# Strassen's weight sums: made once in the mix phase and kept in memory, instead of three times in the up-projection

## The chip, the cores and the metric

The kernel runs on one core of a Trainium2 chip. The time is the device time of one launch in microseconds, taken as the median of a few runs. The profile comes from one further execution that was recorded by the hardware profiler.

## The reference

One decoder layer runs on 2048 prompt positions and 64 sample positions (8 sequences of 8), D_MODEL 1024. The input is normalised and projected; three branches (windowed attention, a spatial-gating MLP, cross-attention into a memory) are each mapped back to 1024 channels, gated and summed; then a ConvFFN follows: an up-projection to 2 x 2816 channels, a causal convolution of width 3 over the positions, a gated GELU, and a down-projection.

```python
gate_logits = ...                                   # 3 x 1024 of the input projection
proj = einsum('blnc,ncd->blnd', branches, w_o)
x = x + rms_norm(sum(sigmoid(gate_logits) * proj, axis=2), post_mix_g)
h = rms_norm(x, pre_ffn_g)
up = einsum('bld,df->blf', h, w_up)                 # 1024 -> 5632
ext = concatenate([conv_past, up], axis=1)
c = conv_b + sum(ext[:, j:j+L] * conv_w[j] for j in range(3))
gate, val = split(c, 2)
f = einsum('blf,fd->bld', gelu(gate) * val, w_down)
x = x + rms_norm(f, post_ffn_g)
```

All of it is in float32. For a product to be as exact as that, each operand is split into a high and a low part, and three matmuls (high x high, high x low, low x high) stand for one.

## The kernel before

The program has four stages, one after the other: stage 1 (branches), the mix phase (gates, branch outputs and their sum), the up phase and the down phase. The 2112 positions are handled in three token groups g of T2 = 704, and 704 is two halves of CW = 352. `split` (L69 to L72) makes the two parts of an operand: ACT casts the source to the high part (L71), and VectorE subtracts that from the source to get the low part (L72).

**Mix phase** (`mix_phase`). For each token group, `proj0` projects branch 0 with four weights; then `branches` goes over n = 0, 1, 2 and op = 0 to 3: two gate weights, and for n > 0 one projection weight, are loaded by `load_w` (512 KB each, DMA issued on the queue of SyncE, SP; split on ACT and VectorE; four weight buffers, three buffers for what is loaded). A gate gemm is 48 matmuls for each half of an `op`, a projection gemm 24, so an `op` has 96 matmuls of 128x352 for n = 0 and 144 for n > 0. `load_br` loads and splits the four tiles of a branch (`bx`), and `post_mix` normalises the sum, adds it to x and stores it.

**Up phase** (`up_phase`). One step of Strassen's algorithm (Winograd's form) halves the rows of the weight, the columns of the weight and the positions, so 7 products do the work of 8. A `Quad` is one (g, f) of 3 token groups and 22 pairs of feature tiles: 66 quads, each of 7 products, each product of 12 matmuls 128x352. For each token group `build_ops` (L915 to L940) loads the activations, scales them on VectorE (L928), makes the four sums t1 to t4 on GpSimd (L936) for each of 4 j, and splits 7 operands for each j: 28 tiles, of 32 buffers. For each quad `build_w` (L942 to L959) loads the raw weight in one DMA of 1024 KB, GpSimd makes the four sums s1 to s4 (L954), and all seven are split: 7 casts on ACT, 7 subtractions on VectorE (tiles `wa` for the raw ones, `ws` for the sums). So each weight is read, summed and split three times, once for each token group.

The products gather in PSUM banks x and y (two buffers each) and w (one). ACT copies partial results out of them (L988 p1, p5, u2, u3; L1024 the last product), `plus` (L1013) adds them up into the tile e: u3 + p5 on GpSimd, the others on VectorE. `conv` (L1042, L1046) does the convolution of the gate half and the value half: one ACT operation and two of VectorE on 704 positions for each; then come Gelu on ACT (L1054), the product on VectorE (L1057) and the store to `act_d`. These run in `act`, called by `end`, and the loop calls `q.first()`, `prev.end()`, `q.middle()`, so that one quad's last product comes after the next one's first.

The order of the instructions on each engine is set by the tile framework's scheduler when the program is built, from the order of the code, the buffers and priorities.

## Time and profile before

| What | Value |
|---|---|
| median of 3 runs | 3266.31 us (3262.56 to 3273.02) |
| profiled execution | 3264.22 us, span of its instructions 3262.4 us |
| mean granted clock of TensorE | 0.965 |
| stages on the span | stage 1 to about 725 us, mix phase to 1680, up phase to 2706, down phase to 3262 |
| busy share | PE 93%, VectorE (DVE) 65%, ACT 43%, GpSimd (POOL) 36% |

A busy time is the sum of an engine's instructions; SP issues the DMAs. PEld is the load of weights into TensorE, which runs beside the matmuls. The granted clock is the share of full speed that the throttle let TensorE have in a stretch. "x" numbers are counts of instructions.

### The profile page before, as it was taken

The numbers are of one execution on the slowest core, as the hardware profiler recorded it, in microseconds if no ns is written. First come the engines' busy times: TensorE is split into PE (matmuls) and PEld (weight loads), VectorE is DVE, ScalarE is ACT, GpSimd is POOL, SyncE is SP. The second block draws the span as 40 slices with busy tenths as digits, with TensorE's granted clock in tenths as the row PEclk, the third lists the DMA queues.
The fourth block names the chain that finished last, engine by engine and source line by source line (L and its number), as shares of the span: only waits on it lengthen the run. The fifth ranks groups of instructions, "written<-read, shape, count | busy, mean of one in ns | idle before, by whom it ended". The sixth has DMA issues, their size and how long they took to land.

```text
span 3262.4 us, 50709 instructions
## 1 busy us (share of the span) xinstructions
PE 3031.9 (93%) x20060; PEld 2962.3 (91%) x20060; DVE 2114.6 (65%) x3013; ACT 1400.7 (43%) x2547; POOL 1185.4 (36%) x1062
## 2 busy tenths in 40 slices
PE   8999999989998999899939999899989997999997
PEld 8999999989998999899938998799979997999997
DVE  6666665544235423632289999999999995555553
ACT  5545564123223212322225555555555554444442
POOL 3221100000111111301167777777789981222221
PEclk9999999999999999899959999999999998999999
DMA  6222233224124212512142223322322226666662
GB/s 201 57 73 74 89 94 84 74 87 145 66 89 160 102 65 89 183 63 74 44 151 100 101 91 105 109 87 105 109 84 105 88 91 232 222 213 202 207 198 103
DMA packets 162894, 376.47 MB, mean 115 GB/s; under 512 B 21520, under 2 KB 94736, under 8 KB 154192
## 3 DMA queue, kind: packets, MB, share of 16 engines
q1 hardware_dynamic: 162656, 373.24, 34.5%
q8 instruction: 157, 2.57, 0.3%
q14 instruction: 81, 0.66, 0.1%
HBM read 315.17 MB, written 58.99 MB: 115 GB/s over the span
## 4 chain that ended last, share of the span: by engine, by line
PE 64%; DVE 21%; issue 8%; ACT 3%; DMA 2%; POOL 1%; SPq 0%; DVEq 0%; ACTq 0%; POOLq 0%
PE ps_g L740 16%; PE ps_d L1121 16%; DVE c L1046 7%; PE ps_p L740 6%; DVE ws L72 4%; PE ps_x L979 4%; PE ps_q L188 3%; PE ps_sv L188 3%; PE ps_up L202 2%; PE ps_mqp L202 2%; DVE wa L72 2%; PE ps_y L979 2%; PE ps_kv L188 1%; DVE m L868 1%; PE ps_w L979 1%
## 5 line engine op out<-in xcount | busy, mean ns | idle before, releaser
L740 PE MATMUL ps_g<-h,w_g 128*128 128x352 f32 x3456 | 570.9, 325 | 16.2 <-ACT m L833 16.2
L740 PEld LDWEIGHTS ps_g<-h,w_g 128*128 128x128 f32 x3456 | 563.0, 191 | 16.6 <-ACT m L833 16.6
L1121 PE MATMUL ps_d<-a,wd 128*128 128x352 f32 x3168 | 514.8, 324 | 16.9 <-ACT a L71 16.1
L1121 PEld LDWEIGHTS ps_d<-a,wd 128*128 128x128 f32 x3168 | 510.9, 190 | 18.2 <-ACT a L71 16.7
L1046 DVE SCALAR_TENSOR_TENSOR c<-e,k_conv_w,c 128x704 f32<-128x704 f32 (+1 forms) x264 | 347.3, 1317 | 10.4 <-ACT c L1042 9.1
L856 POOL TENSOR_TENSOR m<-m,sg 128x704 f32<-128x704 f32 x48 | 94.9, 1977 | 693.0 <-DVE sg L855 531.3
L72 DVE TENSOR_TENSOR ws<-s,ws 128x512 fp32r<-128x512 f32 x264 | 312.4, 1189 | 19.2 <-ACT ws L71 19.1
L740 PE MATMUL ps_p<-b,w_p 128*128 128x352 f32 x1728 | 288.8, 325 | 10.0 <-ACT b L71 7.8
L72 DVE TENSOR_TENSOR wd<-wr,wd 128x1408 fp32r<-128x1408 f32 x96 | 160.3, 1675 | 204.3 <-ACT wd L71 202.6
L740 PEld LDWEIGHTS ps_p<-b,w_p 128*128 128x128 f32 x1728 | 281.6, 190 | 10.5 <-ACT b L71 8.0
L979 PE MATMUL ps_x<-ot,ws 128*128 128x352 f32 x1584 | 279.5, 325 | 4.4 <-ACT u L988 4.3
L979 PEld LDWEIGHTS ps_x<-ot,ws 128*128 128x128 f32 x1584 | 259.8, 191 | 7.1 <-ACT u L988 6.6
L954 POOL TENSOR_TENSOR s<-wr 128x512 f32<-128x512 f32 x132 | 225.5, 1709 | 54.6 <-DMA wr<-in_w_dram 36.2
L850 ACT ACTIVATE sg<-ps_g 128x704 f32<-128x704 f32 x72 | 54.5, 758 | 404.1 <-PE ps_g L740 404.0
L979 PE MATMUL ps_x<-ob,wa 128*128 128x352 f32 x792 | 153.6, 338 | 59.9 <-ACT e L1024 39.6
L979 PEld LDWEIGHTS ps_x<-ob,wa 128*128 128x128 f32 x792 | 131.3, 194 | 76.4 <-ACT e L1024 52.8
L1134 POOL TENSOR_TENSOR acc<-acc,sq 128x352 f32<-128x352 f32 x42 | 43.3, 1031 | 394.4 <-ACT sq L1133 394.4
L72 DVE TENSOR_TENSOR wa<-wr,wa 128x512 fp32r<-128x512 f32 x198 | 185.3, 938 | 0.0
L71 ACT CAST wd<-wr 128x1408 fp32r<-128x1408 f32 x96 | 131.6, 1372 | 105.3 <-PE ps_d L1121 88.5
L72 DVE TENSOR_TENSOR w_g<-ws_g,w_g 128x1024 fp32r<-128x1024 f32 x72 | 98.7, 1371 | 120.2 <-ACT w_g L71 117.1
L979 PE MATMUL ps_y<-ot,ws 128*128 128x352 f32 x792 | 158.9, 335 | 11.8 <-DVE ws L72 7.3
L71 ACT CAST ws<-s 128x512 fp32r<-128x512 f32 x264 | 158.8, 622 | 11.4 <-POOL s L954 9.2
(306 smaller groups left out, 5689.7 us busy)
## 6 DMA issues: line engine op xcount, KB each, us to landing
wr<-in_w_dram SPq DMA_DIRECT2D x66, 1024.0 KB, 4.8
wr<-in_w_dram SPq DMA_DIRECT2D x96, 704.0 KB, 4.2
ws_g<-in_w_dram SPq DMA_DIRECT2D x72, 512.0 KB, 3.3
af<-act_d SPq DMA_DIRECT2D x132, 176.0 KB, 4.3
ws_p<-in_w_dram SPq DMA_DIRECT2D x36, 512.0 KB, 3.2
act_d<-c SPq DMA_DIRECT2D x44, 352.0 KB, 2.3
ws<-in_w_dram SPq DMA_DIRECT2D x26, 512.0 KB, 5.3
bx<-br SPq DMA_DIRECT2D x36, 352.0 KB, 4.0
```

Of the source, the lines that this page charges most:

```text
L71: nc.scalar.copy(out=hi, in_=src)
L72: nc.vector.tensor_tensor(out=lo, in0=src, in1=_f(hi), op=ALU.subtract)
L188: nc.tensor.matmul(ps[:nt, :256], lhsT=h[k // 4][:, a, k % 4, c0 : c0 + nt], rhs=wv[:, b, k], start=(n == 0), stop=(n == 3 * KT - 1),)
L202: nc.tensor.matmul(ps[:, :nt], lhsT=wv[:, a, k, half * P : (half + 1) * P], rhs=h[k // 4][:, b, k % 4, :nt], start=(n == 0), stop=(n == 3 ...
L740: nc.tensor.matmul(ps[:, c, :CW], lhsT=w[:, a, k], rhs=x[:, b, c * CW : (c + 1) * CW], start=(n == 0), stop=(n == tot - 1),)
L850: nc.scalar.activation(v2(sg), ps, AF.Sigmoid)
L856: nc.gpsimd.tensor_tensor(out=mx[o], in0=mx[o], in1=sg, op=ALU.add)
L954: nc.gpsimd.tensor_tensor(out=t, in0=p, in1=m, op=op)
L979: nc.tensor.matmul(ps[:, :CW], lhsT=self.ws[w][:, a, j], rhs=self.ops[o][j][:, b], start=(start and n == 0), stop=(n == 3 * HK - 1), skip_ ...
L1046: nc.vector.scalar_tensor_tensor(out=c[:, :cwid], in0=e[:, t : t + cwid], scalar=cw[:, ft, t : t + 1], in1=c[:, :cwid], op0=ALU.mult, op1= ...
L1121: nc.tensor.matmul(ps[:, :CW], lhsT=w[:, a, k], rhs=acts[i * HF + k][:, b], start=(n == 0), stop=(n == 3 * NF - 1),)
L1134: nc.gpsimd.tensor_tensor(out=acc, in0=acc, in1=sq, op=ALU.add)
```

## The change

In the mix phase a new function `prep` handles one f at a call: it loads the raw weight in four DMAs of 256 KB, makes the four sums on VectorE, splits each (two buffers `pw`), and stores both parts (512 KB) to `sum_d` in memory. It is called after every op of `branches`, until the 22 f are done. In the up phase `build_w` now loads each sum with its two parts (512 KB) from `sum_d` straight into the operand tile, and only the three raw blocks (256 KB each) are loaded and split. The sums t1 to t4 and u3 + p5 go from GpSimd to VectorE. The gate half's convolution is called in `middle` instead of in `act`. Bank x has three buffers and w two. The operands of the second and third token groups are built under the scheduler's lowest priority number. Pools have other sizes and places; `load_w` has two buffers for what is loaded instead of three.

```diff
+    sum_d = [dpool.tile([4, P, 2, 512], F32, tag=f"sumd{f}", name=f"sum_d{f}") for f in range(NF)]
...
-        sp, wp, lp = pool(cm, "s2", 2), pool(cm, "w2", 4), pool(cm, "ld2", 2)
+        hp, wp, lp, sp = pool(cm, "h2", 13), pool(cm, "w2", 4), pool(cm, "ld2", 2), pool(cm, "s2", 2)
...
-            t = lp.tile([P, 1024], F32, tag="ws", name=f"ws_{nm}", bufs=3)
+            t = lp.tile([P, 1024], F32, tag="ws", name=f"ws_{nm}", bufs=2)
...
-        hp, mp, ep = pool(ca, "h2", 15), pool(ca, "mx2", 13), pool(ca, "e2a", 4)
+        mp, ep, pp_ = pool(ca, "mx2", 13), pool(ca, "e2a", 4), pool(ca, "prep", 2)
+        todo = list(range(NF))
+
+        def prep():
+
+            if not todo:
+                return
+            f = todo.pop(0)
+            a = []
+            for i in range(4):
+                t = pp_.tile([P, 512], F32, tag="r", name=f"pr_{f}_{i}", bufs=4)
+                nc.sync.dma_start(out=t, in_=I["w3"][f][:, i * 512 : (i + 1) * 512])
+                a.append(t)
+            a11, a12, a21, a22 = a
+            for i, (o, p, m, op) in enumerate((
+                (a22, a21, a22, ALU.add), (a21, a11, a21, ALU.subtract), (a11, a22, a11, ALU.subtract),
+                (a12, a12, a11, ALU.subtract),
+            )):
+                nc.vector.tensor_tensor(out=o, in0=p, in1=m, op=op)
+                w = pp_.tile([P, 2, 512], F32R, tag="pw", name=f"pw_{f}_{i}")
+                split(w[:, 0], w[:, 1], o)
+                nc.sync.dma_start(out=sum_d[f][i], in_=_f(w))
...
                         if n == 2:
                             sums.add(mx[o])
+                    prep()
...
-        op_, wo, rw, kp = pool(cb_, "ops", 32), pool(cb_, "wo", 10), pool(cb_, "raw", 2), pool(cb_, "k2", 1)
-        ep, cp, lp = pool(cb_, "e2", 6), pool(cb_, "cp", 6), pool(cb_, "ldu", 3)
+        op_, wo, rw, kp = pool(cb_, "ops", 32), pool(cb_, "wo", 12), pool(cb_, "raw", 5), pool(cb_, "k2", 1)
+        lp, ep, cp = pool(cb_, "ldu", 3), pool(cb_, "e2", 6), pool(cb_, "cp", 8)
...
-                    nc.gpsimd.tensor_tensor(out=t, in0=p, in1=src[m] if isinstance(m, str) else m, op=ALU.subtract)
+                    nc.vector.tensor_tensor(out=t, in0=p, in1=src[m] if isinstance(m, str) else m, op=ALU.subtract)
...
         def build_w(f, nm):
-            raw = rw.tile([P, 4, HK * P], F32, tag="raw", name=f"wr_{nm}")
-            nc.sync.dma_start(out=raw, in_=I["w3"][f].rearrange("p (q c) -> p q c", q=4))
-            src = {"a11": raw[:, 0], "a12": raw[:, 1], "a22": raw[:, 3]}
-            for n, p, m, op in (
-                ("s1", raw[:, 2], raw[:, 3], ALU.add), ("s2", "s1", raw[:, 0], ALU.subtract),
-                ("s4", raw[:, 1], "s2", ALU.subtract), ("s3", raw[:, 0], raw[:, 2], ALU.subtract),
-            ):
-                t = rw.tile([P, HK * P], F32, tag="s", name=f"{n}_{nm}", bufs=4)
-                p, m = (src[z] if isinstance(z, str) else z for z in (p, m))
-                nc.gpsimd.tensor_tensor(out=t, in0=p, in1=m, op=op)
-                src[n] = t
+
             ws = {}
-            for n in ("a11", "s1", "a12", "s2", "s4", "s3", "a22"):
+            for n, i in (("a11", 0), ("s1", 0), ("a12", 1), ("s2", 2), ("s4", 3), ("s3", 1), ("a22", 3)):
                 w = wo.tile([P, 2, HK * P], F32R, tag="w", name=f"w{n}_{nm}")
-                split(w[:, 0], w[:, 1], src[n])
+                if n[0] == "s":
+                    nc.sync.dma_start(out=_f(w), in_=sum_d[f][i])
+                else:
+                    raw = rw.tile([P, HK * P], F32, tag="raw", name=f"r{n}_{nm}")
+                    nc.sync.dma_start(out=raw, in_=I["w3"][f][:, i * 512 : (i + 1) * 512])
+                    split(w[:, 0], w[:, 1], raw)
                 ws[n] = w.rearrange("p s (k c) -> p s k c", c=P)
...
-                        [P, 512], F32, tag="q" + bank, name=f"ps_{bank}{self.nm}", bufs=1 if bank == "w" else 2
+                        [P, 512], F32, tag="q" + bank, name=f"ps_{bank}{self.nm}", bufs=3 if bank == "x" else 2
...
                 self.put(plus(nc.vector, u2, y), 0, 1)
+                self.cg, _ = self.conv(0)
                 u3 = self.copy(self.product("x", "s3", "t3", False), "u3")
-                self.put(plus(nc.gpsimd, u3, p5), 1, 1)
+                self.put(plus(nc.vector, u3, p5), 1, 1)
...
-                (cg, cwid), (cv, _) = self.conv(0), self.conv(1)
+                cg, (cv, cwid) = self.cg, self.conv(1)
...
-            ops = build_ops(g)
+            with tc.high_priority(None if g == 0 else 0):
+                ops = build_ops(g)
```

Line numbers after the change are one higher up to L706, 22 to 23 higher in most of the mix phase, and 18 to 23 higher in the up phase: the split of L72 is at L73, L936 at L959, L1013 at L1031, L1046 at L1065.

**The queue of SP where the mix phase begins.** `bx` are loads of a branch, `ws_p` and `ws_g` loads of the weights, `br` stores of stage 1, `pr` loads and `sum_d` stores of `prep`. Before:

```order
L820 DMA bx_0_0_8856<-br_60 128x704
L820 DMA bx_0_1_8861<-br_60 128x704
L729 DMA ws_p_0_0_8876<-in_w_dram 128x1024
L729 DMA ws_p_0_1_8935<-in_w_dram 128x1024
L729 DMA ws_p_0_2_8994<-in_w_dram 128x1024
L802 DMA rbx_9111<-rbc_d 128x704
L705 DMA br_61<-ob_8811 128x4x128
L705 DMA br_61<-ob_8820 128x4x128
L729 DMA ws_p_0_3_9053<-in_w_dram 128x1024
```

After:

```order
L809 DMA pr_0_9301<-in_w_dram 128x512
L809 DMA pr_1_9303<-in_w_dram 128x512
L809 DMA pr_2_9305<-in_w_dram 128x512
L809 DMA pr_3_9307<-in_w_dram 128x512
L819 DMA sum_d_65<-pw_0_9310 128x1024
L809 DMA pr_0_9443<-in_w_dram 128x512
L819 DMA sum_d_65<-pw_1_9315 128x1024
L809 DMA pr_1_9445<-in_w_dram 128x512
L706 DMA br_61<-ob_8833 128x4x128
L819 DMA sum_d_65<-pw_2_9320 128x1024
L809 DMA pr_2_9447<-in_w_dram 128x512
L706 DMA br_61<-ob_8842 128x4x128
```

The first `prep` stands, loads and stores, ahead of the first branch load, and the second one's loads with it. From there on its 22 calls are spread to the second token group's n = 1; 17 of them stand ahead of the second token group's first gate weight.

**The queue of SP where the first token group ends.** `ws_p_0_0` to `ws_p_0_3` are the projection weights of the second token group's `proj0`, `bx_0_3` its last branch tile, without which none of the gemms of `proj0` can finish, `ws_g_0_00` the next gate weight. Before, the branch tiles had been issued (rows ahead of these):

```order
L729 DMA ws_p_0_0_11069<-in_w_dram 128x1024
L729 DMA ws_p_0_1_11128<-in_w_dram 128x1024
L729 DMA ws_p_0_2_11187<-in_w_dram 128x1024
L729 DMA ws_p_0_3_11246<-in_w_dram 128x1024
L729 DMA ws_g_0_00_11464<-in_w_dram 128x1024
```

After:

```order
L730 DMA ws_p_0_2_11548<-in_w_dram 128x1024
L819 DMA sum_d_81<-pw_0_12592 128x1024
L809 DMA pr_0_12782<-in_w_dram 128x512
L819 DMA sum_d_81<-pw_1_12597 128x1024
L809 DMA pr_1_12784<-in_w_dram 128x512
L730 DMA ws_p_0_3_11607<-in_w_dram 128x1024
L819 DMA sum_d_81<-pw_2_12602 128x1024
L809 DMA pr_2_12786<-in_w_dram 128x512
L819 DMA sum_d_81<-pw_3_12607 128x1024
L809 DMA pr_3_12788<-in_w_dram 128x512
L842 DMA bx_0_3_11425<-br_60 128x704
L829 DMA hx_0_11776<-in_xT_dram 128x704
```

The last branch tile now comes behind the last stores of three calls of `prep` (those of `sum_d_79` to `sum_d_81`, of which the rows show the last).

**The order on VectorE in the up phase**, in the second token group (before) and the first (after), from the product of one quad to that of the next. L1046 and L1065 are the convolution, L1057 and L1076 the product. Before:

```order
L1046 SCALAR_TENSOR_TENSOR c_1_1_19643<-e_1_1_19509,k_conv_w,c_1_1_19643 128x704
L72 TENSOR_TENSOR ws_1_3_19754<-s_1_3_19737,ws_1_3_19754 128x512
L1046 SCALAR_TENSOR_TENSOR c_1_1_19649<-e_1_1_19510,k_conv_w,c_1_1_19649 128x704
L1013 TENSOR_TENSOR e_1_2_19656<-p_1_2_19626,ps_w_2_19673 128x352
L72 TENSOR_TENSOR wa_1_3_19757<-wr_3_19729,wa_1_3_19757 128x512
L1013 TENSOR_TENSOR e_1_2_19656<-u_1_2_19699,ps_y_2_19658 128x352
L1046 SCALAR_TENSOR_TENSOR c_1_1_19643<-e_1_1_19509,k_conv_w,c_1_1_19643 128x704
L72 TENSOR_TENSOR wa_1_4_19886<-wr_4_19876,wa_1_4_19886 128x512
L1046 SCALAR_TENSOR_TENSOR c_1_1_19649<-e_1_1_19510,k_conv_w,c_1_1_19649 128x704
L72 TENSOR_TENSOR ws_1_4_19889<-s_1_4_19878,ws_1_4_19889 128x512
L72 TENSOR_TENSOR wa_1_4_19892<-wr_4_19876,wa_1_4_19892 128x512
L1057 TENSOR_TENSOR c_1_1_19643<-c_1_1_19643,c_1_1_19649 128x704
```

After:

```order
L73 TENSOR_TENSOR wa_0_21_19486<-ra_0_21_19487,wa_0_21_19486 128x512
L1065 SCALAR_TENSOR_TENSOR c_0_19_19321<-e_0_19_19261,k_conv_w,c_0_19_19321 128x704 x2
L1031 TENSOR_TENSOR e_0_19_19262<-u_0_19_19337,p_0_19_19276 128x352
L1031 TENSOR_TENSOR e_0_20_19400<-p_0_20_19376,ps_w_20_19417 128x352
L73 TENSOR_TENSOR wa_0_21_19497<-ra_0_21_19498,wa_0_21_19497 128x512
L73 TENSOR_TENSOR wa_1_0_19760<-ra_1_0_19761,wa_1_0_19760 128x512
L1065 SCALAR_TENSOR_TENSOR c_0_19_19393<-e_0_19_19262,k_conv_w,c_0_19_19393 128x704 x2
L1031 TENSOR_TENSOR e_0_20_19400<-u_0_20_19443,ps_y_20_19402 128x352
L1076 TENSOR_TENSOR c_0_19_19321<-c_0_19_19321,c_0_19_19393 128x704
```

Splits of `ws` (weight sums) are gone and the add of u and p (u3 + p5) is new; over many quads a quad has 14 instructions on VectorE before (7 splits, 4 of the convolution, 2 adds, 1 product) and 11 after (3 splits, 4, 3 adds, 1).

## Rows read from the trace of the kernel before

**Rows 1.** The page, part 1: each engine's busy time over the whole program.

```profile
PE 3031.9 (93%) x20060; PEld 2962.3 (91%) x20060; DVE 2114.6 (65%) x3013; ACT 1400.7 (43%) x2547; POOL 1185.4 (36%) x1062
```

**Rows 2.** Stretches: us, length, busy by engine (instructions), granted clock, DMA share, GB/s.

```profile
725.00:1041.00 316.00, 313.35 (x1924) 313.05 (x1924) 128.48 (x123) 99.13 (x121) 31.05 (x16) 0.99 0.35 116
1041.00:1061.00 20.00, 4.86 (x31) 4.55 (x30) 12.65 (x12) 6.11 (x8) 8.60 (x4) 0.59 0.59 189
1680.00:1716.00 36.00, 20.38 (x60) 15.74 (x61) 36.00 (x38) 15.28 (x36) 25.02 (x20) 0.55 0.37 109
1716.00:2706.00 990.00, 914.06 (x5486) 889.45 (x5485) 961.05 (x1029) 554.46 (x1034) 777.02 (x725) 0.98 0.27 97
1760.00:2010.00 250.00, 240.60 (x1476) 235.68 (x1475) 243.60 (x246) 140.72 (x260) 183.84 (x157) 1.00 0.29 103
2010.00:2065.00 55.00, 42.87 (x220) 38.32 (x219) 53.61 (x61) 34.10 (x71) 36.27 (x34) 0.91 0.32 104
2365.00:2402.00 37.00, 25.93 (x121) 23.13 (x120) 37.00 (x42) 19.59 (x40) 26.41 (x23) 0.86 0.21 71
2720.00:3245.00 525.00, 520.12 (x3248) 518.81 (x3248) 266.82 (x275) 217.46 (x321) 97.03 (x87) 0.99 0.61 202
```

**Rows 3.** The waits of PE in the up phase, 1716:2706: us, times, longest.

```profile
PE ps_x L979 <- ACT e L1024: 39.6, 44, 2.4
PE ps_x L979 <- ACT u L988: 10.6, 11, 4.1
PE ps_w L979 <- DVE e L1013: 8.8, 3, 7.6
PE ps_y L979 <- DVE ws L72: 7.3, 2, 4.0
```

**Rows 4.** Timeline of PE, 1900:1912, one quad's products: start, us, operation, wait before.

```profile
1907.66 2.08 PE L979 MATMUL ps_y<-ob,ws 128*128 128x352 f32 x12
1910.41 1.88 PE L979 MATMUL ps_x<-ob,wa 128*128 128x352 f32 x10 [0.67 <-ACT e L1024]
```

**Rows 5.** Timeline of VectorE in the same stretch.

```profile
1900.05 1.99 DVE L1046 SCALAR_TENSOR_TENSOR c<-e,k_conv_w,c 128x704 f32<-128x704 f32 x1
1901.96 0.51 DVE L1013 TENSOR_TENSOR e<-u,ps_y 128x352 f32<-128x352 f32 x1
1902.39 0.68 DVE L72 TENSOR_TENSOR wa<-wr,wa 128x512 fp32r<-128x512 f32 x1
1902.99 0.88 DVE L1057 TENSOR_TENSOR c<-c,c 128x704 f32<-128x704 f32 x1
...
1908.26 0.94 DVE L1046 SCALAR_TENSOR_TENSOR c<-e,k_conv_w,c 128x704 f32<-128x704 f32 x1
```

**Rows 6.** Timeline of ACT in the same stretch.

```profile
1909.23 0.79 ACT L1054 ACTIVATE c<-c 128x704 f32<-128x704 f32 x1 [4.37 <-DVE c L1046]
1909.92 0.43 ACT L1024 COPY e<-ps_x 128x352 f32<-128x352 f32 x1
```

**Rows 7.** The page, part 5: GpSimd's sums of the weights.

```profile
L954 POOL TENSOR_TENSOR s<-wr 128x512 f32<-128x512 f32 x132 | 225.5, 1709 | 54.6 <-DMA wr<-in_w_dram 36.2
```

**Rows 8.** Timeline of PE, 1041:1062, from the first token group to the second.

```profile
1049.33 3.71 PE L93 MATMUL ps_st_mix<-ident,rstd_mix 88*128 88x88 f32 x16 [7.18 <-POOL rstd_mix L90]
1061.12 1.25 PE L740 MATMUL ps_g<-h,w_g 128*128 128x352 f32 x3 [8.08 <-ACT m L833]
```

**Rows 9.** All DMA issues: operation, count, KB each, median us to landing.

```profile
wr<-in_w_dram SPq DMA_DIRECT2D x66, 1024.0 KB, 4.8
wr<-in_w_dram SPq DMA_DIRECT2D x96, 704.0 KB, 4.2
ws_g<-in_w_dram SPq DMA_DIRECT2D x72, 512.0 KB, 3.3
af<-act_d SPq DMA_DIRECT2D x132, 176.0 KB, 4.3
...
out_mkT_dram<-mkT SPq DMA_DIRECT2D x1, 512.0 KB, 6.7
```

More of the change, by code (lines that the diff above doesn't have):

```diff
@@ L98, in tile_decoder_layer @@
     stage1(tc, I, O, br, rbc_d, mhalf, gains, split, PASSES, rstd_rows, ident, ident_r)
-    stage2(tc, I, O, br, rbc_d, x1_d, rs2_d, act_d, gains, split, PASSES, rstd_rows)
+    stage2(tc, I, O, br, rbc_d, x1_d, rs2_d, act_d, sum_d, gains, split, PASSES, rstd_rows)
 def stage1(tc, I, O, br, rbc_d, mhalf, gains, split, PASSES, rstd_rows, ident, ident_r):
@@ L706, in pass_b, with stage2 @@
         h = hn
-def stage2(tc, I, O, br, rbc_d, x1_d, rs2_d, act_d, gains, split, PASSES, rstd_rows):
+def stage2(tc, I, O, br, rbc_d, x1_d, rs2_d, act_d, sum_d, gains, split, PASSES, rstd_rows):
     nc = tc.nc
@@ L788, in mix_phase @@
 def mix_phase(c2, tc, env):
-    (nc, I, br, rbc_d, x1_d, rs2_d, gains, split, pool, sp, lp, load_w, gemm, v2, SumSq) = (
+    (nc, I, br, rbc_d, x1_d, rs2_d, sum_d, gains, split, pool, hp, sp, lp, load_w, gemm, v2, SumSq) = (
         env[n] for n in (
-            "nc", "I", "br", "rbc_d", "x1_d", "rs2_d", "gains", "split", "pool", "sp", "lp", "load_w", "gemm", "v2",
-            "SumSq",
+            "nc", "I", "br", "rbc_d", "x1_d", "rs2_d", "sum_d", "gains", "split", "pool", "hp", "sp", "lp", "load_w",
+            "gemm", "v2", "SumSq",
         )
@@ L890, in up_phase @@
 def up_phase(c2, tc, env):
-    (nc, I, O, x1_d, rs2_d, act_d, gains, split, PASSES, pool, ps2, v2) = (
+    (nc, I, O, x1_d, rs2_d, act_d, sum_d, gains, split, PASSES, pool, ps2, v2) = (
         env[n] for n in (
-            "nc", "I", "O", "x1_d", "rs2_d", "act_d", "gains", "split", "PASSES", "pool", "ps2", "v2",
+            "nc", "I", "O", "x1_d", "rs2_d", "act_d", "sum_d", "gains", "split", "PASSES", "pool", "ps2", "v2",
         )
```

## The prediction

> **What bounds the kernel now.** I read the page's engine times first: TensorE (PE) is busy 3031.9 of 3262.4 us [rows 1], so nothing can gain much except where PE is held up. The table of stretches says where that is [rows 2]. In the mix phase's first group PE is busy 313 of 316 us, in the down phase 520 of 525. In the up phase, 1716 to 2706, PE executes 5486 matmuls in 990 us. What one of them costs without a wait is in the timeline: products of 12 follow each other every 1.92 us (1907.66 starts 1.92 after its predecessor, which shows as 2.08 us because starts overlap), so 0.160 us each [rows 4]. 5486 x 0.160 = 878 us: 112 us of the up phase are lost.
>
> VectorE is the engine that takes them. It is busy 243.6 of 250 us in the steady stretch 1760 to 2010 and all 37 of 37 at the step to the third token group [rows 2]. 246 instructions at 14 a quad are 17.6 quads, so a quad takes 250 / 17.6 = 14.2 us, against 84 x 0.160 = 13.44 us for PE. The waits of PE show the link: 39.6 us in 44 waits for ACT's copy L1024 [rows 3], and that copy stands in ACT's queue behind a Gelu that itself waited 4.37 us for VectorE's convolution [rows 6]. The waits in the rows make 66 us; the rest of the 112 lies in smaller ones and in stretches at a lower granted clock (0.91 and 0.86 at the two steps between token groups [rows 2]).
>
> Why VectorE needs 243.6 / 17.6 = 13.8 us a quad: the same convolution takes 0.94 us at one time and 1.99 at another [rows 5]. GpSimd, whose sums take 1.7 us each [rows 7], is busy 184 of 250 us [rows 2], and I take it that an operation of VectorE with two inputs in SBUF is held up while GpSimd has one. The undisturbed durations are 0.68 (split 128x512), 0.94 (convolution), 0.51 (add 352), 0.88 (product) [rows 5]: 7 x 0.68 + 4 x 0.94 + 2 x 0.51 + 0.88 = 10.4 us, so 3.4 us a quad are contention.
>
> **Up phase, steady.** The change leaves VectorE 3 splits, 4 convolutions, 3 adds and 1 product: 3 x 0.68 + 4 x 0.94 + 3 x 0.51 + 0.88 = 8.2 us, and takes GpSimd's large operations away, so the 8.2 should hold. That is 61% of PE's 13.44: PE becomes the bound. Bank x's third buffer and the earlier gate convolution also take the link over L1024 away. If contention stayed as it is (13.8 / 10.4 = 1.33 times) VectorE would have 10.9 us, still under 13.44, so the conclusion does not hang on it.
>
> **Up phase, between token groups.** The 55 us from 2010 hold 220 matmuls (35 us) and the 37 us from 2365 hold 121 (19 us): 20 and 18 us lost [rows 2]. Afterwards 28 operand tiles must again be split with 32 buffers, so 24 of them wait for the old group's last quad: 24 x 0.51 = 12.2 us and the quad's own 8.2 make 20.4 us of VectorE against 13.44 of PE: about 7 lost at each, 14 together. The 16 sums t now made there (8.2 us) and 8 scalings (7.5 us) would make it 15 more each if all fell there, none if all are ahead; I take them as ahead. For the clock after these and bubbles at a product's start I leave 15 us (before, 112 - 38 = 74 us were lost outside these steps, 66 x 0.8 = 53 of them the quads' own). So 878 + 14 + 15 = 907 us instead of 990: **-83**, between -112 (nothing lost) and -50 (contention or steps stay half).
>
> **Ramp.** From 1680 to 1716 VectorE is busy 36 of 36 us [rows 2]: operands of the first group and the first weights. The sums come to VectorE (16 x 0.51 = 8 us more), four of seven weight splits go (by the order some 8 to 12 of them here, 5 to 8 us less), and 25 us of GpSimd beside it end. I take **-8**, between -12 and +5.
>
> **Down phase, stage 1, gap ahead of down:** the code is the same, and the last quad's tail before the down phase's first loads is as long: 0 each.
>
> **Mix phase: what is added.** 22 calls of `prep`, each 4 sums and 4 subtractions on VectorE (8 x 0.68 = 5.4 us; 120 us in all), 4 casts on ACT, 4 loads and 4 stores on SP's queue, 3.1 MB. VectorE is busy 128 of 316 us in the first group [rows 2]; 17 preps add 93: 221 of 316. Hidden. The memory moves 116 GB/s at a share of 0.35 there [rows 2], 331 GB/s at a full share; 17 x 3.15 MB in some 330 us add 162: 278 GB/s, a share of 0.84. Fits on average, the densest stretches not.
>
> What is not hidden is order. At the start the first branch tile stands behind four stores, each of which needs load, sum and split: 4.3 us for a small load [rows 9] and 1.3 for each sum and split, partly before stage 1 ends: some 4 to 10 us later. At the end of the first group the last branch tile `bx_0_3` stands behind the stores of three preps. With two `pw` buffers a prep takes two rounds of (landing + sum and split): 2 x (3.3 + 1.3) = 9.2 us with the 512 KB row, 2 x (6.7 + 1.3) = 16 with the slowest 512 KB in the trace [rows 9]. Three are 28 to 48 us, against PE work of about 1.5 ops of 144 matmuls (23 us each), 35 us, from the issue of the last gate weight: 0 to 13 us late, in a step that already loses 15 us to other waits [rows 8]. Sum: **+15**, between 0 and +40.
>
> **Sum.** -83 - 8 + 15 = -76. The profiled execution took 3264.2 us (span 3262.4), the median of the runs is 2.1 us higher, less than they differ. 3264.2 - 76 = **3188 us**.
>
> **A rule that speaks against it.** In the up phase one load of 1024 KB a quad becomes three of 256 and four of 512 KB, 2.88 MB with 0.36 MB stored: 3.24 MB in 13.44 us, 241 GB/s. The down phase sustains 202 GB/s at a share of 0.61 with PE at 99%, so 331 GB/s at a full share [rows 2]; 241 is a share of 0.73, and its 96 weight loads and 132 activation loads take 96 x 4.2 + 132 x 4.3 = 971 us to land [rows 9], in a phase of 542 us: they overlap.
> The Trainium skill, "DMA: Bandwidth & Descriptors", section "Anatomy of one DMA", gives a DMA 2.0 us fixed plus its bytes at 436 GB/s, and its "Bandwidth" section asks to batch to at least 1 MiB; applied to DMAs one after another, the down phase's 228 loads would need 669 us, more than that whole phase, so the trace does not bear it out as a serial cost.
>
> **Rivals.**
> 1. *Prep holds up the mix phase* (slower). If the stores land slowly while 278 GB/s are asked for, SP's queue is the bound of the first group, as the weights of the next op stand between stores. The 22 preps stand beside some 400 us of PE's work (313 us of the first group [rows 2] and five ops of the second). All that the change gains elsewhere, 91 us, is used up at 491 / 22 = 22.3 us a prep, a landing of 22.3 / 2 - 1.3 = 9.9 us. At 11 us a prep takes 24.6, 22 of them 541: +141 - 91 = +50, 3314. Against it: the slowest 512 KB landed in 6.7 us [rows 9]. 0.06.
> 2. *Transfers bound the up phase* (no gain). If no more than the 202 GB/s of the down phase can be had beside this traffic, a quad takes 3.24 / 0.202 = 16.0 us, 66 quads 1059 us: +69 - 8 + 15, 3340. Against it the share of 0.61. 0.03.
> 3. *Seven loads one after another.* By the landings of the rows, 7 x 3.3 us and a store are 25 us a quad if none overlapped, 1650 us for the up phase: some 3900. The Trainium skill's rule named above gives 20.6 us for the loads. The overlap in the down phase speaks against it. 0.01.
> 4. *Half the gain.* The steps between groups stay as long as before (38 us lost instead of 14) and the mix takes its +40: 3264 - 59 - 8 + 40 = 3237. For it: the DMA queue is full in the mix, and VectorE now also makes the sums t. 0.20.
> 5. *The change does not reach the bound:* something else than VectorE held PE, and the time stays within 10 us. Against it: VectorE at 97%. 0.03.
> Forecast: 0.67.
>
> **How the numbers follow.** The predicted time is the forecast's 3188. Its own range is 3155 (all of 112 gained but the mix paid) to 3215; the lower end is 3150, the upper takes in rival 4: 3245, which leaves out rivals 1, 2, 3, 5 and a few hundredths of the others. What can be told from no change is 0.3%, 10 us. Faster: forecast and rival 4, 0.87; the same: rival 5 and a little of 1, 0.04; slower 0.09.
>
> **What the profile afterwards would show.** Up phase: VectorE at 60 to 65% of the steady stretch, its convolutions near 0.94 us throughout, GpSimd under a third, PE near 99%, 620 matmuls or more per 100 us (before 1476 in 250, 590 in 100 [rows 2]), DMA share near 0.7. PE's wait for L1024 gone. Steps between groups: 7 to 15 us idle. Mix: new idle time of PE under 20 us in the first group, at its start and its end, none in the third. Wrong if PE waits for `ws` loads in the up phase, if convolutions still take 2 us with GpSimd idle, or if the mix phase is over 40 us longer.

## The result and the profile after

The changed kernel takes 3163.81 us (median of 3 runs, 3162.45 to 3163.89), a ratio of 0.9682 to the kernel before (95% interval 0.9656 to 0.9707): 102 us less. The forecast was 3188 us in a range of 3150 to 3245. The stage marks of the two profiled executions (PE's first matmul of a stage, on the span):

| | before | after | difference |
|---|---|---|---|
| end of stage 1 | 717.6 | 718.8 | +1.2 |
| wait ahead of the mix phase | 7.8 | 12.6 | +4.8 |
| mix phase, to the first matmul of up | 954.7 | 971.6 | +16.9 |
| up phase, to the first matmul of down | 1040.5 | 917.9 | -122.6 |
| down phase to the end | 541.8 | 539.7 | -2.1 |

The stretches of the kernel after (us, length, busy time of PE, PE's weight load, VectorE, ACT and GpSimd with their instructions, granted clock, DMA share, GB/s) answer to [rows 2]:

```profile
725.00:1050.00 325.00, 312.54 (x1914) 311.03 (x1915) 210.31 (x257) 137.71 (x189) 34.54 (x16) 0.97 0.79 279
1050.00:1077.00 27.00, 6.82 (x42) 6.50 (x42) 21.72 (x23) 9.88 (x14) 11.58 (x5) 0.61 0.89 303
1760.00:2010.00 250.00, 250.00 (x1562) 250.00 (x1561) 157.13 (x223) 123.94 (x222) 28.43 (x75) 1.00 0.74 247
2010.00:2065.00 55.00, 53.97 (x333) 52.87 (x332) 47.55 (x79) 31.28 (x59) 21.76 (x16) 1.00 0.82 275
2620.00:3140.00 520.00, 516.06 (x3238) 515.03 (x3239) 266.78 (x275) 216.72 (x319) 97.24 (x86) 0.99 0.61 203
```

In 1760 to 2010 PE is busy all 250 us with 1562 matmuls, 0.160 us each; VectorE has fallen from 244 to 157 us, GpSimd from 184 to 28, and the memory moves 247 GB/s at a share of 0.74. The step to the second token group (2010 to 2065) holds 333 matmuls where it held 220. In the mix phase's first group the memory moves 279 GB/s at 0.79, where it moved 116. The waits of PE in the up phase that were [rows 3] are now:

```profile
PE ps_x L997 <- ACT ob L72: 4.3, 1, 4.3
PE ps_y L997 <- DVE ob L73: 0.7, 1, 0.7
PE ps_x L997 <- ACT u L1006: 0.5, 1, 0.5
PE ps_x L997 <- ACT p L1006: 0.5, 2, 0.2
```

VectorE in 1760 to 2010: the convolution, the split of a raw weight and u3 + p5 (busy us and mean ns of one; after that the idle time before it and what ended that). Before, the convolution, the split of a weight sum and the add that reads PSUM took in this stretch:

```profile
L1046 DVE SCALAR_TENSOR_TENSOR c<-e,k_conv_w,c 128x704 f32<-128x704 f32 x70 | 95.1, 1358 | 0.6 <-ACT c L1042 0.2
L72 DVE TENSOR_TENSOR ws<-s,ws 128x512 fp32r<-128x512 f32 x70 | 90.3, 1294 | 5.8 <-ACT ws L71 5.8
L1013 DVE TENSOR_TENSOR e<-p,ps_w 128x352 f32<-128x352 f32 x18 | 9.2, 509 | 0.0
```

After, the convolution's mean has fallen from 1358 to 951 ns:

```profile
L1065 DVE SCALAR_TENSOR_TENSOR c<-e,k_conv_w,c 128x704 f32<-128x704 f32 x73 | 69.4, 951 | 23.5 <-ACT c L1061 22.3
L73 DVE TENSOR_TENSOR wa<-ra,wa 128x512 fp32r<-128x512 f32 x56 | 38.5, 690 | 57.3 <-ACT wa L72 57.2
L1031 DVE TENSOR_TENSOR e<-u,p 128x352 f32<-128x352 f32 x19 | 10.0, 526 | 6.7 <-ACT u L1006 6.7
```

What the mix phase pays shows at its start, one wait that was 7.8 us:

```profile
731.47 33.04 PE L741 MATMUL ps_p<-b,w_p 128*128 128x352 f32 x192 [12.64 <-ACT w_p L72]
```

and where the second token group begins, two waits that were 7.18 and 8.08 us [rows 8]:

```profile
1062.07 3.72 PE L94 MATMUL ps_st_mix<-ident,rstd_mix 88*128 88x88 f32 x16 [9.62 <-POOL rstd_mix L91]
1076.34 0.95 PE L741 MATMUL ps_g<-h,w_g 128*128 128x352 f32 x2 [10.55 <-ACT m L855]
```

Two more waits stand in that step. The first is new, for the split of the last branch tile, and the second was 4.0 us:

```profile
1021.42 3.89 PE L741 MATMUL ps_p<-b,w_p 128*128 128x352 f32 x12 [4.71 <-ACT b L72]
```

```profile
PE ps_st_x L84 <- DVE ac_x L764: 7.9, 1, 7.9
```

SP's queue itself stood for the splits of `prep` from 990 to 1080 us, 17.9 of these 26.3 us ahead of the load of that last branch tile. It was issued at 1014.15, after PE's last gemm of the first group had ended at 1013.8:

```profile
SPq L819 <- DVE pw L73: 26.3, 15, 6.5
```

The DMAs of the up phase and the stores of `prep` land within 3.8 to 5.1 us by their medians (operation, count, KB, median us):

```profile
ws<-sum_d SPq DMA_DIRECT2D x264, 512.0 KB, 5.1
ra<-in_w_dram SPq DMA_DIRECT2D x198, 256.0 KB, 3.8
sum_d<-pw SPq DMA_DIRECT2D x88, 512.0 KB, 5.0
act_d<-c SPq DMA_DIRECT2D x44, 352.0 KB, 5.1
```

### The profile page after: what moved, and what is told of

Same layout as the page of the kernel before. It is cut to its first block, busy times and chain, and to the rows that moved or that the text cites. A ratio compares the mean times of both kernels' runs of the same rounds, so it can differ in the third digit from the quotient of the medians.

```text
span 3160.7 us, 51575 instructions
## 1 busy us (share of the span) xinstructions
PE 2996.0 (95%) x20060; PEld 2950.8 (93%) x20060; DVE 1821.8 (58%) x3061; ACT 1329.4 (42%) x2371; POOL 547.0 (17%) x662
## 4 chain that ended last, share of the span: by engine, by line
PE 78%; DMA 8%; DVE 7%; issue 3%; ACT 2%; POOL 1%; SPq 0%; DVEq 0%; ACTq 0%; POOLq 0%
PE ps_d L1141 16%; PE ps_x L997 16%; PE ps_g L741 11%; PE ps_y L997 8%; PE ps_p L741 4%; PE ps_w L997 4%; PE ps_q L189 3%; PE ps_up L203 3%; PE ps_sv L189 3%; DMA pr<-in_w_dram 3%; PE ps_mqp L203 3%; DMA sum_d<-pw 2%; PE ps_kv L189 1%; DVE m L891 1%; DVE pw L73 1%
## 5 line engine op out<-in xcount | busy, mean ns | idle before, releaser
L741 PE MATMUL ps_g<-h,w_g 128*128 128x352 f32 x3456 | 574.1, 326 | 18.6 <-ACT m L855 18.6
L741 PE MATMUL ps_p<-b,w_p 128*128 128x352 f32 x1728 | 291.4, 326 | 18.6 <-ACT w_p L72 13.0
L1065 DVE SCALAR_TENSOR_TENSOR c<-e,k_conv_w,c 128x704 f32<-128x704 f32 (+1 forms) x264 | 252.1, 956 | 68.8 <-ACT c L1061 61.7
L73 DVE TENSOR_TENSOR wd<-wr,wd 128x1408 fp32r<-128x1408 f32 x96 | 161.4, 1685 | 206.1 <-ACT wd L72 204.6
L73 DVE TENSOR_TENSOR wa<-ra,wa 128x512 fp32r<-128x512 f32 x198 | 134.9, 689 | 155.5 <-ACT wa L72 154.7
L72 ACT CAST wd<-wr 128x1408 fp32r<-128x1408 f32 x96 | 131.8, 1372 | 109.1 <-PE ps_d L1141 90.7
L1061 ACT ACTIVATE c<-e,k_conv_b,k_conv_w 128x704 f32<-128x704 f32 (+1 forms) x132 | 129.6, 982 | 68.8 <-DVE e L1031 49.0
L72 ACT CAST wa<-ra 128x512 fp32r<-128x512 f32 x198 | 121.8, 624 | 85.9 <-PE ps_y L997 46.2
L73 DVE TENSOR_TENSOR w_g<-ws_g,w_g 128x1024 fp32r<-128x1024 f32 x72 | 98.7, 1371 | 91.9 <-ACT w_g L72 89.3
L1052 POOL COPY tails<-e 128x2 f32<-128x2 f32 x88 | 61.4, 697 | 520.6 <-DVE e L1031 520.4
L997 PE MATMUL ps_w<-ob,wa 128*128 128x352 f32 x792 | 147.9, 323 | 0.7 <-ACT wa L72 0.7
L997 PE MATMUL ps_y<-ot,ws 128*128 128x352 f32 x792 | 146.7, 324 | 0.3 <-DMA ws<-sum_d 0.3
```

Of the source, the lines that this page charges most:

```text
L72: nc.scalar.copy(out=hi, in_=src)
L73: nc.vector.tensor_tensor(out=lo, in0=src, in1=_f(hi), op=ALU.subtract)
L741: nc.tensor.matmul(ps[:, c, :CW], lhsT=w[:, a, k], rhs=x[:, b, c * CW : (c + 1) * CW], start=(n == 0), stop=(n == tot - 1),)
L997: nc.tensor.matmul(ps[:, :CW], lhsT=self.ws[w][:, a, j], rhs=self.ops[o][j][:, b], start=(start and n == 0), stop=(n == 3 * HK - 1), skip_ ...
L1052: nc.gpsimd.tensor_copy(out=tails[:, ft], in_=e[:, T2 : T2 + 2])
L1061: nc.scalar.activation(c[:, :cwid], e[:, 2:ew], AF.Identity, bias=cb[:, ft : ft + 1], scale=cw[:, ft, 2:3])
```

## The experiments

The theory of the prediction, V: in the up phase PE waits because VectorE's time per quad, work and contention with GpSimd, exceeds PE's 13.44 us. Rivals: C, contention alone is the cause; L, the link through ACT's copy L1024 is. Beside these: what in the change is worth how much, and what `prep` costs where. All ratios are to the kernel before, with their 95% interval; "up" is the length of the up phase in the profiled execution, first matmul to the first of the down phase (that of banks_only was its slowest of ten, 3267.91 us).

| run | us | ratio | up |
|---|---|---|---|
| sums_on_vector | 3178.23 | 0.9723 (0.9707 to 0.9740) | 953.3 |
| banks_only | 3259.40 | 0.9977 (0.9966 to 0.9989) | 1037.9 |
| one_prep | 3135.96 | 0.9595 (0.9574 to 0.9617) | 918.2 |
| late_prep | 3144.92 | 0.9616 (0.9598 to 0.9634) | 917.5 |
| gpsimd_load | 3317.66 | 1.0173 (1.0146 to 1.0201) | 1060.6 |
| banks_undone | 3165.23 | 0.9703 (0.9679 to 0.9726) | 922.8 |
| no_store | 3172.06 | 0.9728 (0.9709 to 0.9746) | 949.1 |
| store_in_up | 3145.61 | 0.9644 (0.9619 to 0.9669) | 923.7 |
| gpsimd_four | 3177.59 | 0.9732 (0.9711 to 0.9752) | 936.1 |
| no_priority | 3160.99 | 0.9678 (0.9657 to 0.9699) | 918.1 |
| adds_on_gpsimd | 3173.05 | 0.9717 (0.9692 to 0.9742) | 927.6 |
| late_prep_post | 3127.46 | 0.9579 (0.9566 to 0.9592) | 919.3 |

**sums_on_vector**: the kernel before, GpSimd's additions moved to VectorE and nothing else.

```diff
-                    nc.gpsimd.tensor_tensor(out=t, in0=p, in1=src[m] if isinstance(m, str) else m, op=ALU.subtract)
+                    nc.vector.tensor_tensor(out=t, in0=p, in1=src[m] if isinstance(m, str) else m, op=ALU.subtract)
...
-                nc.gpsimd.tensor_tensor(out=t, in0=p, in1=m, op=op)
+                nc.vector.tensor_tensor(out=t, in0=p, in1=m, op=op)
...
-                self.put(plus(nc.gpsimd, u3, p5), 1, 1)
+                self.put(plus(nc.vector, u3, p5), 1, 1)
```

> The kernel before, with all sums of weights and operands and u3 + p5 on VectorE instead of GpSimd, nothing stored. Theory V (VectorE's whole time per quad, work and contention, must be under PE's 13.44 us): VectorE then has 7 x 0.68 + 4 x 0.68 + 4 x 0.94 + 3 x 0.51 + 0.88 = 13.7 us undisturbed, so it stays the bound: 3226 to 3260 us. Rival C (contention with GpSimd is the whole cause): its convolutions fall from 1.3 to 0.95 us and the up phase falls to some 920 us: 3150 to 3180 us.

3178 us: the rival's number. VectorE did five instructions more a quad and was quicker. Its steady stretch and the step to the second group:

```profile
1760.00:2010.00 250.00, 247.93 (x1542) 246.73 (x1540) 236.43 (x368) 157.02 (x288) 72.29 (x73) 1.00 0.30 109
2010.00:2065.00 55.00, 47.84 (x275) 46.51 (x276) 55.00 (x93) 33.83 (x65) 20.04 (x12) 0.91 0.33 111
```

and its convolution and the split of a sum (1358 and 1294 ns before):

```profile
L1046 DVE SCALAR_TENSOR_TENSOR c<-e,k_conv_w,c 128x704 f32<-128x704 f32 x75 | 70.7, 947 | 2.1 <-ACT c L1042 1.9
L72 DVE TENSOR_TENSOR ws<-s,ws 128x512 fp32r<-128x512 f32 x75 | 50.6, 687 | 1.4 <-ACT ws L71 1.2
```

PE does 1542 matmuls in 250 us, near its rate, with VectorE busy 236. That is 236.4 / (1542 / 84) = 12.9 us a quad, not the 13.7 that I had added up: instructions overlap, and busy time counts an overlap once. The split at 1902.39 takes 0.68 us and the next instruction starts at 1902.99, after 0.60 [rows 5]; 19 instructions at 0.08 are 1.5 us less. Against that the 12.9 hold some 0.7 us a quad for the operands of the next group, which the 13.7 had not. V's condition holds (12.9 is under 13.44, and PE is nearly never late), but my sum was wrong on the side that mattered, so this run does not tell V from C; gpsimd_four does. In the step, where operands come on top, VectorE is busy 55 of 55 us and PE loses 55 - 275 x 0.160 = 11 us.

**banks_only**: the kernel before with the PSUM banks and `conv(0)` in `middle` as in the change.

```diff
-                        [P, 512], F32, tag="q" + bank, name=f"ps_{bank}{self.nm}", bufs=1 if bank == "w" else 2
+                        [P, 512], F32, tag="q" + bank, name=f"ps_{bank}{self.nm}", bufs=3 if bank == "x" else 2
...
+                self.cg, _ = self.conv(0)
...
-                (cg, cwid), (cv, _) = self.conv(0), self.conv(1)
+                cg, (cv, cwid) = self.cg, self.conv(1)
```

> The kernel before, with only the PSUM banks (x 3, y 2, w 2) and the gate half's convolution in middle. Theory V: VectorE stays busy 97%, so PE waits as long in other places: 3255 to 3270 us. Rival L (the wait for ACT's copy L1024 was the cause, 39.6 us in 44 waits): 3220 to 3230 us.

Within 0.3% of before. PE's largest waits in the up phase of this run:

```profile
PE ps_x L979 <- ACT u L988: 37.8, 43, 4.7
PE ps_x L979 <- DVE ob L72: 10.4, 4, 5.2
```

The 39.6 us behind L1024 are gone, and the wait for another of ACT's copies, L988, has grown from 10.6 [rows 3] to 37.8 us: L was a symptom.

**one_prep**: one call of `prep`, whose sums all quads load; the other 21 calls are left out.

```diff
-        todo = list(range(NF))
+        todo = [0]
...
-                    nc.sync.dma_start(out=_f(w), in_=sum_d[f][i])
+                    nc.sync.dma_start(out=_f(w), in_=sum_d[0][i])
```

> The changed kernel with one call of prep instead of 22, and all weight sums loaded from the one that was stored (the up-projection is computed with the wrong sums; the same loads, bytes and matmuls in the up phase). It prices prep in the mix phase. Theory V with my reading of the mix: 16 to 20 us less, 3144 to 3148 us, up phase unchanged at 918. If prep is hidden and the mix is longer for its smaller pools (13 tiles instead of 15, two loads instead of three): 3158 to 3164.

3136 us: the other 21 calls cost 28 us, not 17, by the difference of the two medians. The up phase is the same (918.2), the mix phase 947.2 us. That is also 7.5 less than before the change, while the wait ahead of it (11.4 us) is 3.6 more; why was not tried.

**late_prep**: the calls tied to their place in the mix phase.

```diff
-        def prep():
+        def prep(after):
...
+                if i == 3:
+                    nc.gpsimd.tensor_copy(out=t[:, 0:2], in_=after[:, 0:2])
...
-                    prep()
+                    if 2 <= 4 * n + op <= 9:
+                        prep(mx[2 * op + 1])
```

> The changed kernel with the calls of prep tied to the op they stand behind (a copy of two columns by GpSimd into the fourth raw tile ahead of its load), from op 2 of n = 0 to op 1 of n = 2 of each of the three groups, so that none stands before the first branch tile or in the steps between groups. If the order on SP's queue is what prep costs: 8 to 15 us less than the changed kernel, 3149 to 3156. If its bytes or VectorE's work cost: 3160 to 3170.

3145 us, a little below the expectation; 19 of the 28 us are back with the same bytes and the same work. PE's waits from the start of the mix phase to the second group:

```profile
PE ps_p L741 <- ACT w_p L72: 8.9, 1, 8.9
PE ps_g L741 <- ACT m L857: 8.1, 1, 8.1
PE ps_st_mix L94 <- POOL rstd_mix L91: 5.3, 1, 5.3
```

12.6 is 8.9, 10.6 is 8.1, 9.6 is 5.3, and some 6 us of waits for `proj0`'s operands are gone, 4.7 of them that for the last branch tile. So two thirds of what `prep` cost went with its place. But the run changes two things: each of the three groups now has its share of the calls, and the mix phase's first group moves 200 GB/s where the change has 279. For the order speaks SP's queue in the changed kernel, which stood 26.3 us for `prep` and issued the last branch tile too late, and that beside 279 GB/s the first group's work, from its first gate matmul on, takes 249.5 us where it took 248.5. The density may have a part in the step: that tile took 6.4 us to land, the 36 branch loads 4.4 in the median. No run takes the two apart.

**gpsimd_load**: four additions a quad of constants on GpSimd, in the changed kernel.

```diff
+                for z in range(4):
+                    jk = kp.tile([P, 32, 8, 2], F32, tag="junk", name=f"jk{z}_{self.nm}", bufs=2)
+                    nc.gpsimd.tensor_tensor(out=jk, in0=state[:, 0:32], in1=state[:, 8:40], op=ALU.add)
```

> The changed kernel with four additions 128x512 on GpSimd in every quad, of constants and to a tile that nobody reads: about as much as the weight sums were. If what counts is that VectorE's need stays under PE's 13.44 us a quad: VectorE's operations get slower (convolution from 0.95 to about 1.3 us), its need rises from 8.2 to at most 11 us, PE does not notice: 3160 to 3175 us. If GpSimd beside VectorE holds up PE whatever VectorE's load is: 3190 us or more.

Slower than before, by 1.7%, and not the dose that was meant: nothing holds these additions back, so GpSimd ran them one after another from 1683 us on, 22 us ahead of the up phase's first matmul: 135 in these 250 us, 9.4 for each of the 1203 / 84 = 14.3 quads done:

```profile
1760.00:2010.00 250.00, 208.64 (x1203) 202.83 (x1202) 224.82 (x162) 86.19 (x157) 244.94 (x192) 0.92 0.53 183
```

```profile
L1040 POOL TENSOR_TENSOR jk<-k_state 128x512 f32<-128x512 f32 x135 | 219.8, 1658 | 0.0
```

That is a test of contention at full load. VectorE's convolution, and two additions of the same 352 columns, of which the first has both inputs in SBUF and the second one input in PSUM:

```profile
L1068 DVE SCALAR_TENSOR_TENSOR c<-e,k_conv_w,c 128x704 f32<-128x704 f32 x59 | 129.3, 2191 | 22.0 <-POOL e L1053 20.8 <-ACT c L1064 0.2
...
L1031 DVE TENSOR_TENSOR e<-u,p 128x352 f32<-128x352 f32 x14 | 16.2, 1158 | 0.0
L1031 DVE TENSOR_TENSOR e<-p,ps_w 128x352 f32<-128x352 f32 x15 | 7.6, 509 | 0.0
```

The first takes 1158 ns and the second 509, in the same stretch; in the kernel before, the second took 509 too. Of these rows, only those with two inputs in SBUF are held up. VectorE's need rose from 157.1 / 18.6 = 8.4 to 224.8 / 14.3 = 15.7 us a quad, 0.8 us for each addition, above 13.44, and PE fell to 77% of its rate (1203 of 1562); it came back when the additions were done at 2208 us (619 matmuls from 2200 to 2300). PE waits for none of these additions, so they act through VectorE's time. Some of the loss is of another kind: 20.8 us of VectorE's waits there are for GpSimd's small copies L1053 behind the additions.

The Trainium skill, "SBUF — State Buffer", section "Who interferes with whom", says that a VectorE instruction with two SBUF inputs contends with a GpSimd instruction that reads SBUF and that one with at most one does not, outside the two-port modes; these rows agree.

**banks_undone**: the changed kernel with the banks and `conv(0)` as before.

```diff
-                        [P, 512], F32, tag="q" + bank, name=f"ps_{bank}{self.nm}", bufs=3 if bank == "x" else 2
+                        [P, 512], F32, tag="q" + bank, name=f"ps_{bank}{self.nm}", bufs=1 if bank == "w" else 2
...
-                self.cg, _ = self.conv(0)
...
-                cg, (cv, cwid) = self.cg, self.conv(1)
+                (cg, cwid), (cv, _) = self.conv(0), self.conv(1)
```

> The changed kernel with the PSUM banks and the place of the gate half's convolution as before. If the wait for ACT's copy L1024 was a consequence of a late VectorE: 3160 to 3172 us. If it is a link of its own (0.5 to 0.8 us a quad): 3190 to 3215 us.

3165 us, and its interval overlaps that of the change: with VectorE in time, this part of the change is worth nothing measurable, from this side too.

**no_store**: the changed kernel with `build_w` as in sums_on_vector, no `prep`, and the pools as before.

```diff
-                    prep()
...
+            for n, p, m, op in (
+                ("s1", raw[:, 2], raw[:, 3], ALU.add), ("s2", "s1", raw[:, 0], ALU.subtract),
+                ("s4", raw[:, 1], "s2", ALU.subtract), ("s3", raw[:, 0], raw[:, 2], ALU.subtract),
+            ):
...
+                nc.vector.tensor_tensor(out=t, in0=p, in1=m, op=op)
```

> The changed kernel without stored sums: in the up phase every quad loads its raw weight, makes the four sums on VectorE and splits all seven; the mix phase as before the change. It prices the stored sums with everything else of the change in place. By the run with all sums on VectorE, the steady quad is PE's (VectorE 94% busy, PE 100%), so what the stored sums give lies in the ramp and the two steps between groups, some 25 to 35 us of the up phase, and the mix gives back 17: 3165 to 3182 us. If steps and ramp are short here too, thanks to priority and banks, 3145 to 3160: then the stored sums cost more than they give.

3172 us, as expected. The up phase is 949.1 us against 917.9, so the stored sums are worth 31 us there and cost some 18 in the mix phase and ahead of it (no_store waits 8.4 us there and then takes 957.4). What stays is 0.9728 against 0.9682, about 0.5%; by the two medians it is 8 us, 0.3%.

**store_in_up**: the first token group makes, splits and uses the sums, and stores them; no `prep`, and the mix phase's pools as before.

```diff
+            if g == 0:
+                a11, a12, a21, a22 = (load(n, i) for i, n in enumerate(("a11", "a12", "a21", "a22")))
...
+                    if p is not None:
+                        nc.vector.tensor_tensor(out=o, in0=p, in1=m, op=op)
+                    nc.sync.dma_start(out=sum_d[f][i], in_=_f(parts(n, o)))
+                return ws
```

> The sums are made and split on VectorE by the first token group of the up phase, which uses them at once and stores them; the second and third group load them. The mix phase is as before the change. If the first group runs at PE's rate as the run with all sums on VectorE did: mix phase 17 us shorter than in the changed kernel, up phase up to 10 us longer (ramp): 3146 to 3158 us. If its stores (2 MB a quad beside 1 MB of loads) or VectorE hold up the first group: over 3164.

3145.61 us (3137.58 to 3153.18): no `prep` in the mix phase, an up phase of 923.7 us, and the same time as late_prep within the spread of the runs. The first group runs at PE's rate: 624 matmuls from 1900 to 2000 us, with VectorE 96% busy and 280 GB/s.

**gpsimd_four**: as gpsimd_load, but with inputs that exist only in their quad.

```diff
+                for z in range(4):
...
+                    nc.gpsimd.tensor_tensor(
+                        out=jk, in0=self.e[0][:, 2:514], in1=self.e[0][:, 100:612], op=ALU.add
+                    )
```

> The changed kernel with four additions 128x512 on GpSimd in every quad, which read the quad's own e tile and so can't run ahead of it (in the run with constants GpSimd ran them back to back, 9.4 to a quad, and VectorE's need rose by 7.5 us a quad, 0.8 for each). At 0.8 to 0.9 us each, four cost VectorE 3.4 us, a need of 11 to 12 us under PE's 13.44: 3160 to 3180 us, most of the loss in the steps between groups and the ramp. If any GpSimd work of that size makes PE wait, through the order of the queues, 3200 us or more.

The dose that was meant, in the steady stretch and at the step to the second group:

```profile
1760.00:2010.00 250.00, 250.00 (x1562) 250.00 (x1562) 200.13 (x222) 122.83 (x217) 145.22 (x150) 1.00 0.74 246
2000.00:2100.00 100.00, 93.64 (x565) 91.83 (x564) 94.50 (x123) 51.18 (x96) 57.34 (x53) 0.97 0.73 247
```

```profile
L1040 POOL TENSOR_TENSOR jk<-e 128x512 f32<-128x512 f32 x75 | 104.9, 1418 | 0.0
```

VectorE's need is 200.1 / 18.6 = 10.8 us a quad, 0.6 for each addition of 1.4 us, and PE is not late at all: 1562 matmuls, as without. So contention as such does not hold up PE, which was C's claim. The 14 us that it costs are at the steps: 565 and 574 matmuls from 2000 to 2100 and 2300 to 2400, where the change has 613 and 622. This is V as stated: contention costs nothing until VectorE's need reaches PE's time.

**no_priority**: the changed kernel without that one line.

```diff
-            with tc.high_priority(None if g == 0 else 0):
-                ops = build_ops(g)
+            ops = build_ops(g)
```

> The changed kernel without the priority for the operands of the second and third group. If that is why the steps between groups lose only 2 us of PE instead of the 14 of the runs without stored sums: 3175 to 3190 us, some 10 us more at each step. If it is VectorE's free time: 3160 to 3168.

3161 us: the priority is worth nothing measurable (619 and 622 matmuls in the two steps' windows), which leaves the other reading, that VectorE has time there.

**adds_on_gpsimd**: t1 to t4 and u3 + p5 back on GpSimd.

```diff
-                    nc.vector.tensor_tensor(out=t, in0=p, in1=src[m] if isinstance(m, str) else m, op=ALU.subtract)
+                    nc.gpsimd.tensor_tensor(out=t, in0=p, in1=src[m] if isinstance(m, str) else m, op=ALU.subtract)
...
-                self.put(plus(nc.vector, u3, p5), 1, 1)
+                self.put(plus(nc.gpsimd, u3, p5), 1, 1)
```

> The changed kernel with the sums t1 to t4 and u3 + p5 on GpSimd as before. In the steady quad one GpSimd addition costs VectorE 0.8 us of its spare time: nothing. In the ramp 16 additions of 1.2 us on GpSimd hold up VectorE, which there is the bound, and the chain t1, t2, t4 is longer: 8 to 20 us more; at the two steps 0 to 10 each: 3172 to 3190 us. If contention does not matter outside the steady quad: 3160 to 3170.

3173 us, the up phase 927.6 against 917.9. It is not the ramp as I expected (538 matmuls from 1700 to 1800, the change has 537) but the steps: 588 and 593 matmuls in the two windows of 100 us where the change has 613 and 622, 9 us together.

**late_prep_post**: late_prep, and one more addition moved, in a place where the change left it on GpSimd.

```diff
-                nc.gpsimd.tensor_tensor(out=m, in0=m, in1=x, op=ALU.add)
+                nc.vector.tensor_tensor(out=m, in0=m, in1=x, op=ALU.add)
```

> The late_prep kernel, with the addition of x in post_mix (eight of 128x704 on GpSimd, 2.3 us each) on VectorE too. If GpSimd's two-input work is what makes VectorE's scalings there 2.0 us instead of 0.95, the chain of 8 scalings, 8 additions and 7 sums takes 23 x 0.87 = 20 us instead of 25, and PE's wait of 26.1 us ahead of the up phase falls to 20 to 22: 3136 to 3142 us. If the chain is held by ACT's squares or the loads of x: 3144 to 3148.

3127 us, the fastest run, 1.1 to 1.2% below the changed kernel (by the ratios and by the two medians) and more than expected. `post_mix`'s scalings in late_prep:

```profile
L894 DVE SCALAR_TENSOR_TENSOR m<-m,c_gains,rs_mix 128x704 f32<-128x704 f32 x8 | 15.4, 2000 | 0.0
```

and in this run, with the additions:

```profile
L894 DVE SCALAR_TENSOR_TENSOR m<-m,c_gains,rs_mix 128x704 f32<-128x704 f32 x8 | 7.0, 948 | 0.0
L897 DVE TENSOR_TENSOR m<-m,xr 128x704 f32<-128x704 f32 x8 | 6.8, 887 | 1.7 <-DMA xr<-in_xT_dram 1.7
```

The wait ahead of the up phase fell only from 26.1 to 23.3 us. The larger part came in the second and third group of the mix phase, which run `post_mix` of the group before beside their gates: from its first gate matmul to the end of its gemms, the second took 262.1 and takes 253.5 us, the third 260.9 and 249.1. PE's waits there for the sum of squares of `post_mix` (`ac_x`), 5.4 and 4.2 us, are gone. So are the 6.8 us behind each of them at a granted clock of 0.50 (1.2 of 2.4 GHz), which cost half of their length: 3.4 us. That is the whole of the second group's gain and 7.6 us of the third's 11.8; the rest stays open. The waits ahead of these gates grew, from 8.1 to 12.1 us.

## Why the prediction was right, and where it was off

The sign, the place and the mechanism held: PE was bound by VectorE in the up phase, and afterwards is not. What was off is the size, -102 us instead of -76, and the working shows in which terms.

- **Steady quad: right.** 0.160 us a matmul, VectorE at 157 / 250 = 63% (60 to 65% forecast), convolutions at 0.95, GpSimd at 11%, 0.74 of the DMA (0.73). For bubbles and clock I had left 15 us; 2 to 3 are lost.
- **Ramp: mis-sized, 18 us lost in the forecast and 11 measured.** The first 36 us of the up phase hold 156 matmuls, 25 us of work, where they held 60 [rows 2]. The term is the 8 us that I took for the end of GpSimd's work there, with the sums t and the missing splits about even. In sums_on_vector VectorE takes over the sums t and the weight sums, stores nothing, and still 21 us are lost for 26 (94 matmuls in its first 36 us): the end of GpSimd's work paid for all of these sums and 5 us more. Without stored sums, with the rest of the change but for the pools (no_store, 107 matmuls) 19 are lost, so the stored sums took off the last 8. What each term is worth by itself, no run shows.
- **Steps: mis-sized, 14 us lost in the forecast and 3 measured.** The rule "24 tiles wait for the old group's last quad" took them as all due in one quad. By my reading of the code, which no run tests, PE frees and uses them one product after another. What the runs show is that VectorE's free time decides, some 40% in the change: with the adds of the change back on GpSimd 11 us are lost, with gpsimd_four's additions 18, without stored sums 25.
- **Mix: mis-sized, +15 in the forecast and +21.7 measured** (16.9 in the mix phase and 4.8 ahead of it). The two places were the right ones: the start (4 to 10 forecast, 4.8) and the step to the second group (0 to 13 forecast; from the end of the first group's gemms to the second group's first gate matmul 51.2 us before and 62.5 after, 11.3 more). One wait of 4.7 us is for the last branch tile's split, the one that stands behind the preps. That most of the cost hangs on the calls' place late_prep shows; how much of that is order and how much density, it does not.

Less lost than forecast after the change: ramp 7, steps 11, bubbles and clock 13, together 31 of the 32 us by which the up phase's 123 exceed 83 + 8. The mix took 7 more than forecast, so two errors of opposite sign partly cancel in the total.

The rivals: *prep holds up the mix phase* did not decide, since its stores landed in 5.0 us and not the 9.9 at which it would. *Transfers bound the up phase* fell: 247 GB/s at a share of 0.74 beside a PE that is never late. *One after another* fell with it: four loads of 5.1 us, three of 3.8 and a store of 5.1 are 37 us of landing in each 13.44. By the Trainium skill's fit in "DMA: Bandwidth & Descriptors", section "Anatomy of one DMA", put one after another, the loads alone would have been 20.6 us, an estimate; the page made that fit with DMAs issued from GpSimd, these are issued by SP, and as a cost of each DMA in a row no run here bears it out. *Half the gain* wanted 38 us lost at the steps, and 3 are.

One step was right for a reason that the prediction did not weigh: it priced VectorE's need with the whole change made, 8.2 us, and never with the additions moved and nothing stored. That need is 12.9 us and already under PE's time. The same overlap is in its 10.4 us of undisturbed work: 14 instructions at 0.08 us less make 9.3, so by this estimate contention took 4.5 us of the 13.8, not 3.4. Of the 102 us, sums_on_vector has 87 by moving the additions alone; storing the sums adds 31 in the up phase and gives about 18 back (after against no_store). So the forecast's place and direction were right, while keeping the sums, for which the change was made, is the smaller part of the gain.

## What to carry to other kernels

Ask of an engine that is off the critical path whose instructions it lengthens: moving work from GpSimd to a VectorE that was 97% busy made VectorE quicker, because GpSimd's additions had cost it time, 0.6 to 0.8 us for each in the two runs that added some. Then ask whether the rest of a plan still pays: with that done, keeping the sums in memory was worth 0.3 to 0.5%, and 0.9 to 1.1% once they were made later and more spread out (late_prep against no_store, by the medians and by the ratios). Compare an engine's need with the bound per unit of work, from starts and not from durations, before pricing what lies above it.
